# First norm in a hand-written order with its gain spread by TensorE, the conv result kept as a high/low pair in DRAM, and the up projection with its second accumulator first

## The chip, the cores and the metric

The kernel runs on one core of a Trainium2 chip. Such a core has five engines that work side by side, each through its own list of instructions: PE (TensorE, matmul), DVE (VectorE), ACT (ScalarE), POOL (GpSimd) and SP (SyncE, which here issues nearly all DMAs). The metric is the device time of one execution in microseconds. Lower is better.

## The reference

One transformer block on a sequence of 1024 tokens with 1024 features, all in float32:

```python
h = rms_norm(x, norm1_g)
z = h @ w_in                                 # 1024 x 7168
glu_in, q, k, v, gate_logits = split(z)
a = a_val * sigmoid(a_gate)                  # the halves of glu_in
a = causal_depthwise_conv(a, conv_w, conv_b) # 31 taps
a = silu(rms_norm(a, conv_norm_g))
y_a = a @ w_conv_out
o = dilated_window_attention(rms_norm(q), rms_norm(k), v)   # 16 heads, three window groups mixed
y_b = o @ w_attn_out
g_a, g_b = split(sigmoid(gate_logits + gate_b))
x = x + (g_a * y_a + g_b * y_b) @ w_out
h = rms_norm(x, norm2_g)
u = causal_depthwise_conv(h @ w_up, ffn_conv_w, ffn_conv_b) # 3 taps, width 2 x 2816
x = x + (silu(u_gate) * u_val) @ w_down
```

## The kernel before

Every float32 operand of a matmul is split into a rounded high part and the rest, low: `split` (L74) issues the high as a copy on ACT (L76) and the low as a subtraction on DVE (L77). A product is then three matmuls: high x high, high x low, low x high (L108 to L110). Weights come in pieces of 128 x 1024 (512 KB): `stage` loads one into a ring of four buffers, `wsplit` splits it into rings of four high and four low buffers, and `wpiece` does both.

The program is one long list, written in the order of the stages; a scheduler then puts each engine's instructions in an order that follows their dependences and the program order. Memory is handed out in pools, and a tile that takes over memory of an earlier one waits for that one's last user, a DMA included.

- First norm (L197 to L224). The gain g1 is loaded as a broadcast to 128 partitions (`gb1`). For each of eight tiles of 128 tokens: Square with a running sum on ACT, mean and epsilon on DVE, power -0.5 on POOL (`rstd_of`, L98), a scale on DVE (L223), eight transposes on PE (L190), two splits into `hT`.
- GLU (L227 to L238). Per channel of 128 a gate product `glug` and a value product `gluv`, 48 matmuls each.
- q, k, v products, meanwhile the depthwise conv on DVE (`conv_branch`, L242): 31 instructions of 128 x 1024 for each of eight channels.
- Gate products, drawn from the generator `gate_steps` (L146) as cover for PE: 24 steps before the conv's sum of squares, 16 before its spread (`psr`, L333), and 52 behind the loop L336 to L340, which scales each conv channel (DVE), applies Silu (ACT) and writes it to DRAM, `da`, by a DMA on SP's queue (`COVER`, L36). Each gate piece is loaded as `raw_gt`, split into `hi_gt` and `lo_gt`; ACT brings the result out as `gs` (L151).
- Attention (L345 to L470). `head` loads q, kh, kl, mask m and v of a head (L133); `score` (L378), `flip` and `weigh` work on it a head half at a time. Between them `fill` takes steps from `side_work`: the remaining gates, then the projection `ya` of the conv branch, whose input `aT` is read back from `da` in eight pieces and split again by `load_split` (L165).
- Merge, output projection and second norm (L473 to L543): `wo` products by tile of 128 tokens, the norm's steps, transposes (`transpose_raw`, L509) two tiles later.
- Up projection (L557 to L659). The product of 1024 x 1024 by 1024 x 256 (f-th columns of value and gate) is made with seven products of half-size blocks in place of eight. The blocks of the normed input are b11, b12, b21, b22, their sums t1 to t4 (`sums`, L594, with subtractions on POOL), each split. `up_first` makes the first two products into the accumulators X and Z, `up_sums` the sums of the weights, `up_rest` the remaining five products, into X and Y, and the conv and Silu.
- Down projection (L664 on), likewise in blocks.

## Time and profile before

| | |
|---|---|
| time, median of 3 runs | 1813.47 us (1812.62 to 1814.06) |
| profiled execution | 1811.43 us |
| its span, from first to last instruction | 1809.6 us |
| mean granted clock of PE | 0.991 of full speed |
| busy: PE, DVE, ACT, POOL | 1765.8, 1318.8, 771.6, 195.8 us |
| instructions | 22474 |
| HBM read, written | 190.03 MB, 66.06 MB |

All times within the profile count from the start of the span. A timeline row gives an instruction's start and duration, then engine, line (L76 is line 76 of the kernel), operation, tile written <- tiles read, shape and number of instructions, and in brackets how long the engine stood idle before it and what it then waited for. "SPq" and "ACTq" mark the issue of a DMA. The landing time is from the issue to the DMA's end. Durations of PE's rows are those of single matmuls, which overlap; how far apart the starts are is what one costs.

### The profile page before, as it was taken

To read this page: it belongs to the slowest core of one execution; us is meant where nothing else is said; L and a number is where in the kernel's file an instruction comes from. 1 tells how busy PE (TensorE), PEld (TensorE's weight loads), DVE (VectorE), ACT (ScalarE), POOL (GpSimd) and SP (SyncE) were. 2 spreads that over 40 slices of the span, in tenths; PEclk is the share of its full clock that TensorE was granted. 3 is DMA by queue.
4 is the path that set the end of the run, shared out by engine and by line. 5 is a ranking of instruction groups with operands and counts; after the bars stand their busy time and mean duration, and the time that the engine had idled before them with its cause. 6 is when DMAs were issued, how large, how long until landed. Compare 5 with 4: busy or idle time off the path is not lost.

```text
span 1809.6 us, 22474 instructions
## 1 busy us (share of the span) xinstructions
PE 1765.8 (98%) x8244; PEld 1461.9 (81%) x8244; DVE 1318.8 (73%) x1798; ACT 771.6 (43%) x1202; POOL 195.8 (11%) x197
## 2 busy tenths in 40 slices
PE   7999999999999999999999999989999999999999
PEld 5888888888887888887888878768888888878887
DVE  5999999999735655666654543787777777789863
ACT  4111132232245656666655332545444554543441
POOL 1000133133002122222210000210000000000000
PEclk9999999999999999999999999999999999999999
DMA  5111145345549456666527543313222222389851
GB/s 203 59 47 47 41 134 163 116 134 157 157 173 246 145 158 175 180 165 179 164 70 279 169 160 133 104 48 107 80 82 81 71 95 91 116 303 335 298 180 47
DMA packets 142063, 257.57 MB, mean 142 GB/s; under 512 B 11265, under 2 KB 60545, under 8 KB 141953
## 3 DMA queue, kind: packets, MB, share of 16 engines
q1 hardware_dynamic: 141808, 255.61, 43.8%
q8 instruction: 65, 1.06, 0.3%
q10 hardware_dynamic: 144, 0.52, 0.1%
q14 instruction: 46, 0.37, 0.1%
HBM read 190.03 MB, written 66.06 MB: 142 GB/s over the span
## 4 chain that ended last, share of the span: by engine, by line
PE 53%; DMA 4%; DVE 4%; issue 1%; ACT 1%; SPq 1%; POOLq 0%; POOL 0%; DVEq 0%; ACTq 0%
PE xz L550 5%; PE xz L551 5%; PE xz L552 5%; PE dx L703 5%; PE dy L703 5%; DMA gg<-dya 2%; PE pp L400 2%; PE y L550 2%; PE y L552 2%; PE y L551 2%; PE ya L108 2%; PE ya L109 2%; PE ya L110 2%; PE o L408 2%; PE wo L126 1%; PE wo L127 1%
## 5 line engine op out<-in xcount | busy, mean ns | idle before, releaser
L253 DVE SCALAR_TENSOR_TENSOR cacc<-apad,pk,cacc 128x1024 f32<-128x1024 f32 x240 | 297.7, 1274 | 0.7
L125 PE MATMUL qkv<-hi_qkv,hT 128*128 128x512 f32 x384 | 151.8, 396 | 0.0
L127 PE MATMUL qkv<-hi_qkv,hT 128*128 128x512 f32 x384 | 150.0, 391 | 0.0
L126 PE MATMUL qkv<-lo_qkv,hT 128*128 128x512 f32 x384 | 149.4, 390 | 0.0
L389 DVE CUSTOM_DVE_ANT_0 p<-s,m 128x128 f32<-128x128 f32 (+7 forms) x128 | 95.1, 750 | 62.7 <-PE pp L400 39.0
L77 DVE TENSOR_TENSOR pl<-pp,ph 128x512 fp32r<-128x512 f32 x192 | 103.1, 549 | 49.1 <-ACT ph L76 48.6
L393 POOL TENSOR_SCALAR p<-p,st 128x128 f32<-128x128 f32 (+7 forms) x128 | 94.9, 748 | 335.5 <-DVE st L392 211.9
L76 ACT ACTIVATE ph<-pp 128x512 fp32r<-128x512 f32 x192 | 91.3, 487 | 92.2 <-PE pp L400 89.3
L649 DVE SCALAR_TENSOR_TENSOR u<-u,pk 128x1023 f32<-128x1023 f32 (+1 forms) x88 | 112.3, 1279 | 18.9 <-ACT u L647 18.5
L101 POOL TENSOR_TENSOR rs<-ss,mhalf 128x8 f32<-128x8 f32 (+1 forms) x40 | 80.3, 2010 | 353.1 <-DVE ss L100 353.0
L391 ACT ACTIVATE p<-p,st 128x128 f32<-128x128 f32 (+7 forms) x128 | 99.0, 776 | 14.6 <-DVE st L389 12.9
L108 PE MATMUL gate<-hT,hi_gt 128*128 128x512 f32 x256 | 101.8, 398 | 0.0
L109 PE MATMUL gate<-hT,hi_gt 128*128 128x512 f32 x256 | 100.8, 394 | 0.0
L110 PE MATMUL gate<-hT,lo_gt 128*128 128x512 f32 x256 | 100.3, 393 | 0.0
L400 PE MATMUL pp<-ident,p 128*128 128x128 f32 x576 | 94.4, 277 | 0.0
L127 PEld LDWEIGHTS qkv<-hi_qkv,hT 128*128 128x128 f32 x384 | 72.0, 188 | 15.3
L126 PEld LDWEIGHTS qkv<-lo_qkv,hT 128*128 128x128 f32 x384 | 72.2, 188 | 14.5 <-DVE lo_qkv L77 0.3
L125 PEld LDWEIGHTS qkv<-hi_qkv,hT 128*128 128x128 f32 x384 | 72.2, 188 | 14.0
L400 PEld LDWEIGHTS pp<-ident,p 128*128 128x128 f32 x576 | 69.5, 142 | 10.0 <-issue 0.2
L384 PE MATMUL s<-kh,q 128*128 128x512 f32 (+1 forms) x192 | 69.7, 368 | 7.3 <-DVE st L389 4.8
L408 PE MATMUL o<-ph,v 128*128 128x512 f32 x192 | 73.1, 381 | 3.6 <-ACT ph L76 1.8
L409 PE MATMUL o<-pl,v 128*128 128x512 f32 x192 | 70.5, 369 | 1.6 <-DVE pl L77 1.5
(269 smaller groups left out, 4610.4 us busy)
## 6 DMA issues: line engine op xcount, KB each, us to landing
wr<-w_down SPq DMA_DIRECT2D x45, 512.0 KB, 5.7
gr<-dff SPq DMA_DIRECT2D x62, 256.0 KB, 5.2
raw_qkv<-w_qkv SPq DMA_DIRECT2D x24, 512.0 KB, 3.9
raw_uv<-w_up SPq DMA_DIRECT2D x22, 512.0 KB, 3.3
raw_ug<-w_up SPq DMA_DIRECT2D x22, 512.0 KB, 3.3
dff<-u SPq DMA_DIRECT2D x22, 512.0 KB, 2.6
dv<-v SPq DMA_DIRECT2D x16, 512.0 KB, 3.2
raw_gt<-w_ch SPq DMA_DIRECT2D x16, 512.0 KB, 4.8
```

The costliest lines, as they stand in the source:

```text
L108: pe.matmul(o, hi[:, k, :], ah[:, k, :], start=(k == 0), stop=False)
L109: pe.matmul(o, hi[:, k, :], al[:, k, :], start=False, stop=False)
L110: pe.matmul(o, lo[:, k, :], ah[:, k, :], start=False, stop=(k == KT - 1))
L125: pe.matmul(ps, ah, hi[:, k % 2, :], start=(k == 0), stop=False)
L126: pe.matmul(ps, ah, lo[:, k % 2, :], start=False, stop=False)
L127: pe.matmul(ps, al, hi[:, k % 2, :], start=False, stop=(k == KT - 1))
L253: dve.scalar_tensor_tensor(out=acc, in0=a[:, j : j + T], scalar=w(j), in1=acc, op0=ALU.mult, op1=ALU.add)
L400: pe.transpose(pp[:, qb * P : (qb + 1) * P], pts[qb][:, kt * P : (kt + 1) * P], ident)
L550: pe.matmul(o, wh[:, k, :], bh[:, k, :], start=(start and k == 0), stop=False, skip_group_check=not start)
L551: pe.matmul(o, wh[:, k, :], bl[:, k, :], start=False, stop=False, skip_group_check=not start)
L552: pe.matmul(o, wl[:, k, :], bh[:, k, :], start=False, stop=(k == 3), skip_group_check=not start)
L703: pe.matmul(banks[n], a[:, c], b[:, d], start=(start and i == 0 and m == 0), stop=(stop and i == nf - 1 and m == 2), skip_group_check=True)
```

## The change

Three stages are rewritten; the matmuls stay the same, but for two.

First norm and first GLU channel: g1 comes as one row of 4 KB and is spread over the partitions by two matmuls with ones. ACT, DVE and PE follow an order written by hand: four Squares first, powers a tile ahead of the scales, and the products of the first channel, gate and value for one half of the tokens at a time, are taken high x high first, in between the transposes of the second half.

Conv result: after Silu each channel is split into a high and a low tile in the ring `t4` (four buffers), and both are written to DRAM, `da[0]` and `da[1]`. `aT` is then fetched in four DMAs of 2 MB, with no split behind them.

Second norm and up projection: an order written by hand for ACT, DVE and PE from the last norm tiles to the first up products; the first two up weights are loaded and split ahead of it; all block sums are on DVE, none on POOL. In `up_rest` the products into Y come ahead of those into X, and the two buffers of `u` are swapped.

```diff
-    da = dr.tile([P, KT, T], F32, name="da")
+    da = [dr.tile([P, KT, T], F32R, name=f"da{a}") for a in range(2)]
...
-        gb1 = p1.tile([P, D], F32, tag="csq", bufs=1, name="gb1")
-        act.dma_start(gb1, bass.AP(tensor=g1.tensor, offset=g1.offset, ap=[[0, P], [1, D]]))
+        g1r = p1.tile([1, D], F32, tag="csq", bufs=1, name="g1r")
+        act.dma_start(g1r, g1.unsqueeze(0))
...
-                wfirst = [wpiece(w_ch[8], "g0"), wpiece(w_ch[0], "v0")]
+                wfirst = [(c, n, stage(w_ch[c], n)) for c, n in ((8, "g0"), (0, "v0"))]
...
-            act.activation(xs, xx, AF.Square, accum_out=ss)
-            rstd_of(rs, ss, D, ss)
-            dve.scalar_tensor_tensor(out=xs, in0=xx, scalar=rs, in1=gb1, op0=ALU.mult, op1=ALU.mult)
-            transpose_split(hT, xs, tt)
...
+        gb1 = p1.tile([P, D], F32, tag="sqacc", bufs=1, name="gb1")
+        xn = [t4(f"xs_{tt}") for tt in range(4)]
+        st1 = p1.tile([P, 2, 8], F32, name="st1")
+        tps = {}
+
+        def squares(tt):
+            if tt >= 4:
+                xn.append(t4(f"xs_{tt}"))
+            act.activation(xn[tt], xt[tt], AF.Square, accum_out=st1[:, 0, tt : tt + 1])
+
+        def spread1(tt):
+            rstd_of(st1[:, 1, tt : tt + 1], st1[:, 0, tt : tt + 1], D, st1[:, 0, tt : tt + 1])
+
+        def scaled(tt):
+            dve.scalar_tensor_tensor(out=xn[tt], in0=xt[tt], scalar=st1[:, 1, tt : tt + 1], in1=gb1,
+                                     op0=ALU.mult, op1=ALU.mult)
+
+        def turned(tt):
+            for kk in range(2):
+                ps = third[:, kk * 512 : kk * 512 + 512] if tt == 2 else bank_ps(f"tp_{tt}_{kk}")
+                for j in range(4):
+                    k = kk * 4 + j
+                    pe.transpose(ps[:, j * P : (j + 1) * P], xn[tt][:, k * P : (k + 1) * P], ident)
+                tps[tt, kk] = ps.rearrange("p (a b) -> p a b", a=4)
...
+        HH, HL, LH = ((0, 0),), ((0, 1),), ((1, 0),)
+        with tc.manual_schedule(engines={ENG.Activation, ENG.DVE, ENG.PE}):
+            ps = [bank_ps(f"gb_{kk}") for kk in range(2)]
+            for kk in range(2):
+                pe.matmul(ps[kk], ones[0:1, :], g1r[:, kk * 512 : kk * 512 + 512], start=True, stop=True)
+            for tt in range(4):
+                squares(tt)
+            dve.tensor_copy(gb1[:, 0:512], ps[0])
+            spread1(0)
+            dve.tensor_copy(gb1[:, 512:1024], ps[1])
+            spread1(1)
+            for tt in range(4):
+                scaled(tt)
+                turned(tt)
+                if tt < 2:
+                    spread1(tt + 2)
+                if tt == 2:
+                    both(0, 0)
+            both(0, 1)
+            both(1, 0)
+            both(2, 0)
...
+            act.activation(hl[0][0], wraw[0], AF.Copy)
+            both(3, 0)
+            act.activation(hl[1][0], wraw[1], AF.Copy)
+            wlow(0)
+            wlow(1)
+            a, b = range(4), range(4, 8)
+            first_pair(0, a, HH, 0)
+            first_pair(0, a, HH, 1)
+            first_pair(0, a, HL + LH, 0)
+            first_pair(0, a, HL + LH, 1)
+            squares(4)
+            spread1(4)
...
+            glu0[1] = big_ps("glugv_1")
+            both(6, 1)
+            ends = both(7, 1)
...
-            sp.dma_start(da[:, c, :], ct)
+            pair = [t4(f"a{h}_{c}", F32R) for h in range(2)]
+            split(*pair, ct)
+            for h in range(2):
+                spill(da[h][:, c, :], pair[h])
         for _ in range(COVER[2]):
             next(gates)
 
 
     with tc.tile_pool(name="ph2", bufs=1) as p2:
+        def take(aT, half):
+            for h in range(2):
+                fetch(aT[h][half], da[h][:, :, half * 512 : half * 512 + 512])
+
         def side_work():
             for t in gates:
                 if t == "half":
                     aT = hb_tiles(hb1, "aT")
-                    load_split(aT, da, 0, "a")
+                    take(aT, 0)
                 yield
-            load_split(aT, da, 1, "a")
+            take(aT, 1)
...
                 gemm_tok(ps, mT, wpieces, tt)
-                dve.tensor_tensor(out=x2[:, cs], in0=ps, in1=x2[:, cs], op=ALU.add)
-                sp.dma_start(dx2[tt][:, cs], x2[:, cs])
-                act.activation(ps, x2[:, cs], AF.Square, accum_out=ss2[:, tt, j : j + 1])
+                if j == 1 and tt == 7:
+                    break
+                add_rest(j, tt, x2, ps)
...
-            pool.tensor_tensor(out=t1, in0=b12[:, :, q], in1=b11[:, :, q], op=ALU.subtract)
-            dve.tensor_tensor(out=t3, in0=b22[:, :, q], in1=b12[:, :, q], op=ALU.subtract)
-            keep("t3", t3, q)
-            dve.tensor_tensor(out=t3, in0=t3, in1=b11[:, :, q], op=ALU.add)
-            keep("t2", t3, q)
-            keep("t1", t1, q)
...
+        pre = [stage(w_up[f], f"uv{f}") for f in range(2)]
+        pre = [(v, wsplit(v, f"uv{f}")) for f, v in enumerate(pre)]
+        t2 = [p4r.tile([P, 1024], F32, tag="st", bufs=2, name=f"cb_t2_{i}").rearrange("p (a b) -> p a b", a=4)
+              for i in range(2)]
+        order = tc.manual_schedule(engines={ENG.Activation, ENG.DVE, ENG.PE})
+        order.__enter__()
         transpose_raw(*tails.pop(0))
+        add_rest(1, 7, x2, ps)
+        transpose_raw(*tails.pop(0))
+        q0, q1 = cols
+        less(t13[0], b12[:, :, q0], b11[:, :, q0])
+        s7 = spread(7)
+        high2("t1", t13[0], q0)
+        less(t2[0], b22[:, :, q0], t13[0])
+        scale2(x2, s7)
+        low2("t1", t13[0], q0)
+        v0, xz0 = up_first(0, pre[0])
+        transpose_raw(x2, 7)
         assert not tails
+        weights = up_sums(0, v0)
+        next(weights)
+        ups = [up_first(1, pre[1])]
 
     with tc.tile_pool(name="ph4", bufs=1) as p4:
-        for n in ("b22", "t4"):
-            blocks[n] = p4.tile([P, 2, 4, 512], F32R, name=f"blk_{n}")
-        ups = [up_first(1)]
-        sums(cols[1])
-        for q in cols:
-            keep("b22", b22[:, :, q], q)
-        for i, q in enumerate(cols):
-            pool.tensor_tensor(out=t2[i], in0=b21[:, :, q], in1=t2[i], op=ALU.subtract)
-            keep("t4", t2[i], q)
-        blk = {n: (t[:, 0], t[:, 1]) for n, t in blocks.items()}
+        half4 = lambda pl, n, **k: pl.tile([P, 4, 512], F32R, name=f"blk_{n}", **k)
+        blocks["b22"] = half4(p4, "b22h"), half4(p4, "b22l")
+        high2("b22", b22[:, :, q0], q0)
+        less(t13[1], b12[:, :, q1], b11[:, :, q1])
+        high2("t1", t13[1], q1)
+        less(t2[1], b22[:, :, q1], t13[1])
+        low2("t1", t13[1], q1)
+        high2("b22", b22[:, :, q1], q1)
+        s4 = [four(t) for t in wsplit(v0[:, 512:], "s4_0")]
+        low2("b22", b22[:, :, q0], q0)
+        low2("b22", b22[:, :, q1], q1)
+        for q, t in zip(cols, t2):
+            high2("t2", t, q)
+        for q, t in zip(cols, t13):
+            less(t, b22[:, :, q], b12[:, :, q])
+        for q, t in zip(cols, t2):
+            last = low2("t2", t, q)
+        order.__exit__(None, None, None)
+        sw, gw, _ = next(weights)
+        ready = [(v0, xz0, sw, gw, s4)]
+        with tc.issue_after(last.ins):
+            for q, t in zip(cols, t13):
+                high2("t3", t, q)
+                low2("t3", t, q)
+            blocks["t4"] = half4(p4, "t4h"), half4(p4r, "t4l", tag="t13", bufs=1)
+            for t, q in zip(t2, cols):
+                less(t, b21[:, :, q], t)
+                high2("t4", t, q)
+                low2("t4", t, q)
+        blk = blocks
...
-            u = hb2.tile([P, 4, T], F32, tag=f"hb{f % 2}0", name=f"u_{f}")
+            u = hb2.tile([P, 4, T], F32, tag=f"hb{(f + 1) % 2}0", name=f"u_{f}")
             uv, ug, cv, cg = u[:, 0], u[:, 1], u[:, 2], u[:, 3]
             p5 = cst.tile([P, 512], F32, tag="f2", bufs=2, name=f"p5_{f}")
-            X, Z = xz[:, 0:512], xz[:, 512:1024]
+            X, Z = xz
             Y = bank_ps(f"y_{f}")
             t0, t1 = slice(0, 512), slice(512, 1024)
             (sh, sl), (gh, gl) = sw, gw
             act.activation(uv[:, t0], X, AF.Copy)
             dve.tensor_tensor(out=uv[:, t0], in0=Z, in1=uv[:, t0], op=ALU.add)
+            product(Y, sh[:, 0:4], sl[:, 0:4], *blk["t1"], True)
+            act.activation(p5, Y, AF.Copy)
+            s4h, s4l = s4 if f == 0 else [four(t) for t in wsplit(s4, f"s4_{f}")]
+            product(Y, s4h, s4l, *blk["b22"], False)
             product(X, sh[:, 4:8], sl[:, 4:8], *blk["t2"], False)
             act.activation(uv[:, t1], X, AF.Copy)
-            product(Y, sh[:, 0:4], sl[:, 0:4], *blk["t1"], True)
-            act.activation(p5, Y, AF.Copy)
             product(X, gh[:, 0:4], gl[:, 0:4], *blk["t3"], False)
             dve.tensor_tensor(out=ug[:, t1], in0=X, in1=p5, op=ALU.add)
-            s4h, s4l = [four(t) for t in wsplit(s4, f"s4_{f}")]
-            product(Y, s4h, s4l, *blk["b22"], False)
             dve.tensor_tensor(out=uv[:, t1], in0=Y, in1=uv[:, t1], op=ALU.add)
```

More of the change, by code (lines that the diff above doesn't have):

```diff
@@ L227, in block_kernel @@
+        for ks in (a, b):
+            for which in range(2):
+                first_pair(1, ks, HH + HL + LH, which)
+        with tc.issue_after(ends[1].ins):
+            dve.tensor_tensor(out=qkg, in0=pk[:, C_QG : C_QG + 1], in1=pk[:, C_KG : C_KG + 1], op=ALU.mult)
+            dve.tensor_scalar(qkg, qkg, DH ** -0.5, None, op0=ALU.mult)
+        with tc.issue_after(ends[0].ins), tc.issue_after(ends[1].ins):
+            wsecond = [wpiece(w_ch[9], "g1"), wpiece(w_ch[1], "v1")]
         apad = []
```

164 lines of the change are left out of this document (107 added, 57 removed).

## The prediction

> **What bounds the kernel now.** I read the page first: busy times and the slices.
>
> ```profile
> PE 1765.8 (98%) x8244; PEld 1461.9 (81%) x8244; DVE 1318.8 (73%) x1798; ACT 771.6 (43%) x1202; POOL 195.8 (11%) x197
> ...
> PE   7999999999999999999999999989999999999999
> ```
>
> TensorE (PE) is busy 1765.8 us of a span of 1809.6, so 43.8 us of idle, and some time at a low clock, are all that an edit can win unless it removes matmuls; this one adds two small ones. The time is in a few seams, which the windows view shows (columns: stretch, length, busy time of PE, PE weight load, DVE, ACT, POOL, granted PE clock, DMA share, GB/s).
>
> ```profile
> core 0: us, PE busy (x) PEld busy (x) DVE busy (x) ACT busy (x) POOL busy (x), PEclk, DMA share, GB/s
> 0.00:20.00 20.00, 6.95 (x32) 5.57 (x32) 10.82 (x17) 13.01 (x23) 3.65 (x18) 0.92 0.93 357
> 550.00:600.00 50.00, 48.80 (x253) 40.94 (x253) 28.75 (x84) 30.20 (x68) 13.93 (x20) 0.94 0.82 228
> 800.00:820.00 20.00, 17.13 (x87) 14.19 (x86) 14.97 (x35) 15.31 (x30) 5.16 (x7) 0.89 0.90 258
> 1150.00:1200.00 50.00, 40.76 (x181) 32.08 (x181) 47.90 (x46) 27.87 (x38) 14.03 (x6) 0.93 0.22 72
> ```
>
> 13.05 us idle lie in the first 20 us (the first norm), 2.87 at 800 to 820 (before the conv branch's output projection, ya), 9.24 at 1150 to 1200 (second norm into the up projection), where DVE is busy 47.90 of 50. The change works at these three seams, and it puts new work before a fourth: the start of attention near 547. Between the seams PE is full, so time won at one reaches the end unless a later seam takes it back.
>
> The profiled execution took 1811.43, 2.04 below the median of 1813.47; I sum against the former and add 2 at the end.
>
> **Part 1, the first norm (gain).** The timelines of PE, ACT, DVE and POOL (columns: start, duration, what, in brackets the idle time before and its releaser), then the landing of the broadcast gain (size, median), that of the eight conv spills da (shortest, median, longest), and the rate of all DMA in 40 slices of the first 20 us:
>
> ```profile
> 9.41 4.03 PE L190 MATMUL tp<-ident,xs 128*128 128x128 f32 x16 [9.41 <-DVE ss L100]
> 20.18 0.80 PE L108 MATMUL glug<-hT,hi_g 128*128 128x512 f32 x1 [0.48 <-ACT hT L76]
> 23.94 0.39 PE L109 MATMUL glug<-hT,hi_g 128*128 128x512 f32 x1
> 48.21 0.50 PE L108 MATMUL glug<-hT,hi_g 128*128 128x512 f32 x1
> ...
> 5.99 1.06 ACT L221 ACTIVATE xs<-x 128x1024 f32<-128x1024 f32 x1 [3.55 <-DMA x<-x]
> ...
> 8.07 1.28 DVE L223 SCALAR_TENSOR_TENSOR xs<-x,rs,gb 128x1024 f32<-128x1024 f32 x1 [0.75 <-POOL rs L101]
> 18.13 1.22 DVE L77 TENSOR_TENSOR lo_v<-raw_v,hi_v 128x1024 fp32r<-128x1024 f32 x1
> ...
> 7.48 0.56 POOL L101 TENSOR_TENSOR rs<-ss,mhalf 128x1 f32<-128x1 f32 x1 [6.04 <-DVE ss L100]
> ...
> 506.43 0.61 PE L333 MATMUL psr<-dg,ones 128*128 128x128 f32 x4
> 546.79 0.39 PE L109 MATMUL gate<-hT,hi_gt 128*128 128x512 f32 x1
> 547.02 0.39 PE L110 MATMUL gate<-hT,lo_gt 128*128 128x512 f32 x1
> ...
> gb<-g ACTq DMA_DIRECT2D x1, 512.0 KB, 5.5
> ...
> DMA to landing us min/median/max: 2.6/3.1/7.0
> ...
> GB/s 0 0 0 98 205 229 270 311 336 401 311 401 434 402 418 426 418 418 418 418 426 418 418 418 418 434 410 418 426 410 434 434 393 391 428 437 401 426 410 434
> ```
>
> Today the 512 KB broadcast runs ahead of x. At 418 GB/s that is 1.25 us; with a 4 KB row in its place the x tiles land that much earlier, and the first Square starts at 4.74 instead of 5.99. From Square to power took 1.49 (7.48 - 5.99), from power to scale 0.59 (8.07 - 7.48): by x alone the first scale could start at 6.8. The gain comes through two fp32 matmuls: psr's four of 128 columns took 0.61 at the full clock, so with their tail 0.9 for 512 columns, and 1.7 at the head's clock (the eight steps from 20.18 to 23.94 are 0.47 each, against 0.23 between 546.79 and 547.02), and two copies, of which the last, some 0.7 (a little over half of 1.22), stands behind them. If the row g1r lands 2.6 after its issue near 0.7, as the quickest of da's, that is 3.3 + 3.4 + 0.7 = 7.4, which I take; with the broadcast's 5.5 it would be 10.3. Four scales then follow, each tile's power beside the scale before: 4 x 1.28 and 0.6 for the small steps (read and multiply, within the 0.43 that 1.49 leaves beside the Square), 13.1. With four transposes and one high the first product starts near 15.5, against 20.18. The weight splits and tiles 4 to 7 then lie beside PE work: the 48 products of tiles 0 to 3 for the first channel take 48 x 0.23 and some 2 for the clock, 13 us, while the last x lands at 4.74 + 9 x 1.25 = 16.0. So no later stall. Gain 5 (4 to 6; 2 if g1r lands last): the second channel's first product moves from 48.21 to about 43.2. From there to 500 PE is full, and the gain lasts.
>
> What speaks against it is the power of one tile on POOL beside the scale of another on DVE. Where a power met a split on DVE (two inputs from SBUF) at the second norm, it was stretched:
>
> ```profile
> 1158.24 1.40 POOL L101 TENSOR_TENSOR s<-s,mhalf 128x1 f32<-128x1 f32 x1 [9.12 <-DVE s L100]
> ```
>
> 1.40 against 0.56. In the new head the powers of tiles 2 and 3 are asked for just as a scale starts. If each waits the scale out and then runs, the next scale starts some 0.65 late (0.56 and a hand-over), 1.3 in all, and the gain is 3.7 instead of 5. That is the second rival below; for the sum I keep 5, as three of the four scales may find the power done. The Trainium skill, "SBUF — State Buffer" (Terms, shared port pair), has it as a rule: DVE and GpSimd lock the port pair that they share for a whole instruction, and the loser is blocked until its end. By that rule the head gains 3.7; the 1.40 agrees with it.
>
> **Part 2a, the conv pair before attention (loss).** The timelines of PE, ACT and SP, and SP's waits (total, times, longest):
>
> ```profile
> 549.63 0.77 PE L384 MATMUL s<-kh,q 128*128 128x128 f32 x2 [2.22 <-DMA kl<-dk]
> ...
> 547.22 1.06 ACT L76 ACTIVATE hi_gt<-raw_gt 128x1024 fp32r<-128x1024 f32 x1 [4.48 <-PE gate L109]
> 548.18 0.67 ACT L151 ACTIVATE gs<-gate,pk 128x512 f32<-128x512 f32 x1
> ...
> 531.24 2.23 SPq L340 DMA_DIRECT2D da<-cacc x2
> 539.58 0.52 SPq L133 DMA_DIRECT2D q<-dq x1
> ...
> SPq L133 <- DMA da<-cacc: 4.7, 2, 3.5
> ```
>
> The last gate product ends at E = 547.4 (547.02 + 0.39). Head 0's loads reuse the memory of the conv tiles, so SP issues the first (539.58) only when the last da spill has landed; the spill went out by 533.5. The first score comes 10.05 after the first load, 2.2 after E: nearly in time, because the last spill follows straight on the last Silu.
>
> In the changed order eight highs (ACT, 1.06 as hi_gt) and eight lows (DVE, 1.22) come between Silu and spill, 16 spills go out instead of 8, and a ring of four buffers allows two pairs in flight, so each pair waits for the spills of the pair two before. What decides is the order: on ACT, the high of channel 6 stands behind that hi_gt, and the high of channel 7 behind the last gs. hi_gt stood 4.48 for the gate weights' use on PE, that is until E - 0.2; gs waits for the last gate product itself. So, after E: hi_gt to 0.9, high 6 to 1.9, gs to 2.5, high 7 to 3.5, low 7 (1.22) to 4.7, spill issued. It lands 2.6 to 7.0 later; behind six other transfers of the same queue I take 4.5: E + 9.2. SP holds head 0's loads, and all behind them, for it. The first score came 10.05 after the first load; with less on the DMA, down to 7. I take 8.5: E + 17.7, against E + 2.2: loss 15.5 (bounds: 4.7 + 2.6 + 7 - 2.2 = 12 and 4.7 + 7 + 10.05 - 2.2 = 19.5). PE has nothing else here: the gate cover ahead is as long as before, and the later gate work is woven between scores. The idle costs no more clock than before: 0.94 over 550 to 600 is a cold start already.
>
> **Part 2b, the pair read back (gain).** The PE timeline, and the operations on the tile aT (count, shortest, median and longest ns, first and last start):
>
> ```profile
> 814.45 0.33 PE L408 MATMUL o<-ph,v 128*128 128x128 f32 x1 [1.30 <-ACT ph L76]
> 816.32 0.47 PE L409 MATMUL o<-pl,v 128*128 128x128 f32 x1 [1.54 <-DVE pl L77]
> 820.02 0.63 PE L108 MATMUL ya<-aT,hi_co 128*128 128x512 f32 x1
> ...
> L76 ACT ACTIVATE aT<-raw_a x8: 1042/1059/1070, 760.0 to 813.2; 128x1024 fp32r<-128x1024 f32 x8
> L77 DVE TENSOR_TENSOR aT<-raw_a,aT x8: 1214/1220/1225, 761.2 to 814.8; 128x1024 fp32r<-128x1024 f32 x8
> ```
>
> The second four of these splits, up to 816, stand ahead of the last head's ph and pl, for which PE waits 1.30 + 1.54; the clock of 0.89 over these 20 us is another 2. The splits go; four 2 MB fetches replace the eight loads; the w_co loads move from 812 into the heads before. The last head's chain keeps some wait. Gain 4.5 (3 to 6). The fetches take some 5 us of the DMA's time each and go through SP's queue ahead of head loads, which are a head early: nothing, or up to 2 at a DMA share of 0.90.
>
> **Part 3, second norm into up (about nothing).** PE and POOL timelines and DVE's groups of 1156 to 1200:
>
> ```profile
> 1179.88 0.80 PE L551 MATMUL y<-blk_t,hi_s 128*128 128x512 f32 x1 [4.70 <-DVE blk_t L77]
> ...
> 1169.94 3.05 POOL L599 TENSOR_TENSOR cb_t<-h2raw,h2raw 128x1024 f32<-128x1024 f32 x1 [3.56 <-ACT h2raw L516]
> ...
> L540 DVE SCALAR_TENSOR_TENSOR x<-x,s,gb 128x1024 f32<-128x1024 f32 x2 | 4.7, 2344 | 0.0
> L602 DVE TENSOR_TENSOR cb_t<-cb_t,h2raw 128x1024 f32<-128x1024 f32 x2 | 4.0, 2004 | 0.0
> L77 DVE TENSOR_TENSOR lo_s<-raw_uv,hi_s 128x512 fp32r<-128x512 f32 x2 | 3.6, 1788 | 0.0
> L571 DVE TENSOR_TENSOR s<-raw_ug 128x512 f32<-128x512 f32 x2 | 3.4, 1716 | 0.0
> ```
>
> The four POOL subtractions go to DVE: 4 x 1.22 = 4.9 more. Each of them had stretched one DVE operation; against 1.28, 1.22, 0.68 and 0.68 undisturbed the four groups hold 2.1 + 1.6 + 2.2 + 2.0 = 8 too much, which comes back. DVE, the bound here, has 3 less. But the order written by hand makes waits of its own: the last norm tile's transposes wait for its sum, power and scale; the second half's t2, t3 and t4 splits come ahead of the sums for f = 1, whose s1 products come right behind f = 0's b22. Going through the instructions in the new order with these durations I get PE waits of 0.6, 1.1, 6.0, 0.8 and 1.3, 9.8 in all beside some 1.5 at the last transposes, against 9.24 idle today; and PE's matmuls are then further on. Net gain 1, between -1.5 and 3. The swap of the u buffers and Y before X in every later f moves nothing while PE is full.
>
> **Sum.** -5 + 15.5 - 4.5 - 1 = +5 on 1811.43, 1816.4; with 2 for the median 1818.5. Its own range: loss 12 to 19.5, gains 13 to 8, so 1813 to 1823.
>
> **Rivals.**
> Faster: the spill tail drains within the gates. The pairs are only 8 x 1.06 on ACT and 8 x 1.22 on DVE, some 10 us side by side, and today's last spill goes out 14 before E; were ACT not held by hi_gt and gs, the last would land by E, the loss would be 0 to 6, and the time 1803 to 1809. Against it is the order on ACT and the 4.48. It decides at whether high 7 runs before E. Chance 0.15.
> The lock: head gain 3.7, 1820. Chance 0.15.
> A wash: tail at its lower bound (12), head 6, ya 6 and transition 1: 1812.5 after the median's 2. Chance 0.13.
> Worse: the DMA backs up. 16 spills are 8.4 MB, 20 us at 418 GB/s, beside gate loads and spills; with landings at 7 and loads at 10 (19.5), a late g1r (gain 2) and ya 3: 1811.4 + 19.5 - 2 - 3 + 2 = 1828. Chance 0.12. It decides at a last da landing later than 7 after issue.
> The change doesn't do what it says, because g1r lands as late as the broadcast did: inside the ranges above.
>
> **Numbers.** Forecast 0.45. 0.2% of this time, 3.6 us, is what a measurement can tell from no change; so faster is below 1809.8, slower above 1817.1. Faster: 0.15 + 0.05 of the wash = 0.2. Same: 0.08 of the wash and 0.12 of the forecast's lower end = 0.2. Slower: 0.33 + 0.15 + 0.12 = 0.6. The range, 1808 to 1825, takes in the wash and the near ends of the faster and the worse case.
>
> **What would show it.** First product at 15.5 and the second channel's at 43: part 1 right. PE idle of 12 to 18 between the last gate matmul and the first score, released by a DMA of head 0, with the last da spill issued some 5 after the last gate: part 2a right; the first score within 5 of the gates' end would refute it and make the whole faster. No wait over 1 for ph and pl before ya: 2b. One PE wait near 6 for hi_s of f = 1: part 3. If every term is as given but the total is off, a clock or a DMA wait elsewhere was missed.

## The result, and the profile after

The changed kernel takes 1836.21 us (median of 4 runs, 1832.62 to 1836.77), against 1813.05 (4 runs, 1811.24 to 1814.06) for the kernel before on the same chip: a ratio of 1.0125, 95% interval 1.0107 to 1.0142. It is slower, as predicted, but by 23 us instead of 5, and outside the range. The profiled execution took 1832.62, its span is 1830.8, 21.2 longer than before.

First the busy times of the page after; then the windows that answer to those of before:

```profile
PE 1771.1 (97%) x8248; PEld 1460.8 (80%) x8248; DVE 1317.3 (72%) x1805; ACT 772.6 (42%) x1203; POOL 183.9 (10%) x193
```

```profile
0.00:20.00 20.00, 14.29 (x53) 9.77 (x54) 13.03 (x20) 13.33 (x22) 5.14 (x19) 1.00 0.87 339
550.00:600.00 50.00, 34.05 (x163) 27.89 (x164) 20.24 (x58) 21.04 (x48) 9.85 (x14) 0.76 0.73 196
1150.00:1200.00 50.00, 41.59 (x199) 33.13 (x198) 40.49 (x48) 28.08 (x41) 4.07 (x4) 0.95 0.22 74
```

The work is the same; the idle has moved. PE is busy 14.29 of the first 20 us instead of 6.95, but from 550 to 600 it is busy 34.05 at a clock of 0.76, where it was 48.80 at 0.94. PE's waits in the changed kernel (total, times, longest; rows with a part in the argument):

```profile
PE s L503 <- DMA kh<-dk: 22.1, 1, 22.1
...
PE y L681 <- ACT hi_s L76: 5.7, 1, 5.7
PE dx L868 <- ACT gh_b L76: 3.0, 1, 3.0
PE xz L681 <- ACT u L803: 2.7, 2, 1.6
...
PE dx L868 <- ACT u L808: 1.4, 1, 1.4
```

One wait, before the first score of attention, is 22.1, where it was 2.2 before: a difference nearly as large as the whole loss. The waits for `u` and `gh_b` lie in the last quarter, where the prediction had put nothing at all.

To find where time comes and goes I follow the same matmul through the traces: its start less its start in the kernel before. In the table a term of the sum is the step from one column to the next; times at the top are those of before. (psr: spread of the conv's norm. score 0 and s_2_3: the first and a later score of attention. ya: in the first half of the conv's projection. wo: the middle of the output projection. y_4, y_20: last product into Y for f = 4 and 20. dy: late in the down projection. At each of the last five the same number of products has run before it in every run, but for the four matmul records that spread the gain.)

| run | psr 506.4 | score 0 549.6 | s_2_3 589.7 | ya 884.2 | wo 1110.9 | y_4 1262.4 | y_20 1567.0 | dy 1791.4 |
|---|---|---|---|---|---|---|---|---|
| after | -6.3 | +13.6 | +17.4 | +12.6 | +10.5 | +8.6 | +12.4 | +20.9 |
| e1 head only | -6.5 | -5.6 | -5.3 | -5.9 | -2.1 | -0.8 | -0.8 | -0.8 |
| e2 pair only | +1.5 | +22.2 | +26.3 | +21.3 | +21.9 | +21.9 | +21.9 | +22.3 |
| e3 up only | -0.1 | +1.1 | +2.0 | +2.3 | +0.8 | -0.5 | +2.9 | +15.8 |
| e4 u unswapped | -6.4 | +13.7 | +16.9 | +11.8 | +10.2 | +12.2 | +12.2 | +12.5 |
| e5 low in place | -6.3 | +8.6 | +12.8 | +8.3 | +6.9 | +5.2 | +9.9 | +16.7 |
| e6 swap only | +0.3 | +0.9 | +0.8 | +0.8 | +0.7 | 0.0 | +1.9 | +6.0 |
| e7 head and pair, new order | -6.4 | +13.7 | +17.0 | +12.2 | +10.3 | +10.3 | +10.3 | +10.3 |
| e8 all, both mended | -6.0 | +14.1 | +17.8 | +12.8 | +10.4 | +13.1 | +13.1 | +13.6 |
| e9 double spill | -0.1 | +12.0 | +16.4 | +15.4 | +19.0 | +18.9 | +18.9 | +19.4 |
| e10 high only | -6.3 | +2.1 | +4.9 | +0.1 | -1.3 | -2.1 | +2.5 | +10.0 |
| e11 X first | -6.8 | +13.5 | +16.5 | +11.2 | +14.3 | +12.9 | +14.8 | +21.0 |
| e12 head and up, unswapped | -6.4 | -6.5 | -6.5 | -7.3 | -6.7 | -3.9 | -3.9 | -3.4 |

The changed kernel's row reads: head -6.3, start of attention +23.7, ya -4.8, transition -1.9, up projection +3.8, start of the down projection +8.5. The step from ya to wo, -2.1, is no term: it lies between -2.4 and +3.8 in the other rows without regard to the edits (e1 +3.8, e9 +3.6, e11 +3.1), a seam that varies from run to run. In e1 and e9 PE waits 4.2 and 4.0 at the start of the output projection for its split weights, against 2.8 before and 1.0 after; over the 20 us from there the granted clock is 0.83 and 0.85, in the other two 1.00. So a single profile is good to about 4 us, and the medians of several runs decide.

**The head.** Timelines of PE, DVE and POOL, changed kernel:

```profile
2.32 3.75 PE L254 MATMUL gb<-g1r,ones 1*128 1x512 f32 x4 [2.32 <-DMA g1r<-g]
6.91 1.29 DVE L217 SCALAR_TENSOR_TENSOR xs<-x,st,gb 128x1024 f32<-128x1024 f32 x1
6.94 0.55 POOL L100 TENSOR_TENSOR st<-st,mhalf 128x1 f32<-128x1 f32 x1 [0.78 <-DVE st L99]
9.12 1.28 DVE L217 SCALAR_TENSOR_TENSOR xs<-x,st,gb 128x1024 f32<-128x1024 f32 x1
9.28 1.53 POOL L100 TENSOR_TENSOR st<-st,mhalf 128x1 f32<-128x1 f32 x1 [0.85 <-DVE st L99]
10.85 1.28 DVE L217 SCALAR_TENSOR_TENSOR xs<-x,st,gb 128x1024 f32<-128x1024 f32 x1 [0.36 <-POOL st L100]
16.20 1.20 PE L246 MATMUL glugv<-hT,whi_g 128*128 128x512 f32 x4 [0.96 <-ACT hT L233]
41.70 0.39 PE L107 MATMUL glug<-hT,hi_g 128*128 128x512 f32 x1
```

The row g1r is there at 2.32, the first scale starts at 6.91, the first product at 16.20 instead of 20.18, the second channel's at 41.70 instead of 48.21. Between the first two scales lie 2.21 instead of 1.28: in the order written by hand the small step for tile 2 stands ahead of the second scale, and it waits 0.84 for tile 2's Square, which waits 1.33 for its x to land. The fourth scale, at 12.65, ends at 13.93.

**The start of attention.** Timelines of PE, ACT, DVE and SP of the changed kernel:

```profile
540.77 0.39 PE L109 MATMUL gate<-hT,lo_gt 128*128 128x512 f32 x1
563.23 0.76 PE L503 MATMUL s<-kh,q 128*128 128x128 f32 x2 [22.07 <-DMA kh<-dk]
...
540.97 1.06 ACT L76 ACTIVATE hi_gt<-raw_gt 128x1024 fp32r<-128x1024 f32 x1 [3.53 <-PE gate L108]
542.32 1.06 ACT L76 ACTIVATE a<-cacc 128x1024 fp32r<-128x1024 f32 x1 [0.29 <-DMA da<-a]
543.28 0.67 ACT L150 ACTIVATE gs<-gate,pk 128x512 f32<-128x512 f32 x1
545.45 1.06 ACT L76 ACTIVATE a<-cacc 128x1024 fp32r<-128x1024 f32 x1 [1.50 <-DMA da<-a]
...
546.70 1.23 DVE L77 TENSOR_TENSOR a<-cacc,a 128x1024 fp32r<-128x1024 f32 x1 [1.91 <-DMA da<-a]
...
545.06 3.27 SPq L129 DMA_DIRECT2D da<-a  x3
554.36 0.51 SPq L132 DMA_DIRECT2D q<-dq  x1
```

Who waited for the spills to land there, in the view of the tensor da (us, times), and SP's own wait for the last (total, times, longest):

```profile
  DVE a L77: 5.9, 4
  ACT a L76: 3.3, 3
```

```profile
SPq L132 <- DMA da<-a: 5.8, 1, 5.8
```

and the group of the eight spills before (issue shortest, median and longest in ns, first and last start):

```profile
L340 SPq DMA_DIRECT2D da<-cacc x8: 319/320/1277, 523.5 to 532.6; - x8
```

The last gate product ends at E = 541.2 (540.77 + 0.39). On ACT the order is the one that the prediction had worked out: hi_gt, the high of channel 6, gs, the high of channel 7. But the ring is full: the last two highs wait 0.29 and 1.50 for the landing of the earlier spills whose buffers they take, and the last low, which waits for a buffer too, follows at 546.70. The last three spills are issued at 545.06, 546.53 and 547.96 (the row merges them); each issue takes SP 0.32 to 0.43, and between them SP waits for high and low. The sixteen spills land 2.6 to 7.8 us after their issue, in the median 6.0; the last at 554.08, 6.1 after. The first load of head 0 goes out at 554.36, the first score starts at 563.23, E + 22.1. Granted clock in the ten us from the first score on, before and after (columns as in the windows of the prediction):

```profile
549.60:559.60 10.00, 8.77 (x30) 6.70 (x31) 5.40 (x19) 5.52 (x13) 3.20 (x6) 0.67 1.03 268
```

```profile
563.20:573.20 10.00, 7.72 (x19) 5.57 (x20) 2.37 (x12) 3.69 (x9) 2.13 (x4) 0.50 1.03 260
```

The granted clock in the ten us after a wait of 2.22 was 0.67, after one of 22.07 it was 0.50. That is a part of the 3.8 between score 0 and s_2_3: over that whole stretch the mean granted clock is 0.92 for 40.1 us before and 0.88 for 43.9 after, which makes some 2 us by estimate, and PE is idle 2.8 there instead of 1.2.

**Up and down projection.** Waits of ACT for the writing of `u` to DRAM from 1190 to 1600, before and after:

```profile
ACT u L631 <- DMA dff<-u: 4.8, 4, 2.3
```

```profile
ACT u L796 <- DMA dff<-u: 15.2, 6, 4.0
```

The end of the up projection, timelines of PE and SP in the changed kernel, and SP's wait there; then the timeline of SP at the same place before:

```profile
1606.29 0.39 PE L868 MATMUL dx<-hi_a,early 128*128 128x512 f32 x1
1611.73 0.39 PE L681 MATMUL xz<-blk_t4h,hi_s3g 128*128 128x512 f32 x1
...
1614.64 0.34 SPq L876 DMA_DIRECT2D res<-dx  x1
1617.58 4.50 SPq L841 DMA_DIRECT2D gr<-dff  x7
```

```profile
SPq L876 <- PE xz L683: 8.3, 1, 8.3
```

```profile
1594.71 1.76 SPq L711 DMA_DIRECT2D res<-dx  x4
1596.52 4.62 SPq L676 DMA_DIRECT2D gr<-dff  x7
```

The last X product of f = 21 (`t4`, 12 matmuls) now stands behind 24 products of the down projection. The loads `res` wait 8.3 for it in SP's queue, and the loads `gr` behind them go out 11.3 after the first down product (1617.58 - 1606.29); before, they went out 2.0 after it (1596.52 against 1594.47). PE then waits 3.0 for `gh_b` and 1.4 for `u`. Every run with the buffers swapped has these 24 products ahead of the last X product and the `gr` loads 10.2 to 11.3 after the first down product; every run with them unswapped has 0 and 2.0 to 2.1.

### The profile page after: what moved, and what is told of

Same layout as the page of the kernel before. It is cut to its first block, busy times and chain, and to the rows that moved or that the text cites. A ratio compares the mean times of both kernels' runs of the same rounds, so it can differ in the third digit from the quotient of the medians.

```text
span 1830.8 us, 22492 instructions
## 1 busy us (share of the span) xinstructions
PE 1771.1 (97%) x8248; PEld 1460.8 (80%) x8248; DVE 1317.3 (72%) x1805; ACT 772.6 (42%) x1203; POOL 183.9 (10%) x193
## 4 chain that ended last, share of the span: by engine, by line
PE 50%; DMA 5%; DVE 4%; issue 1%; ACT 1%; SPq 1%; DVEq 0%; ACTq 0%
PE xz L681 5%; PE xz L683 5%; PE xz L682 5%; PE dx L868 5%; PE dy L868 3%; PE pp L519 2%; PE y L681 2%; PE y L682 2%; PE y L683 2%; DMA gg<-dya 2%; PE ya L107 2%; PE ya L108 2%; PE ya L109 2%; PE wo L125 2%; PE wo L126 2%; PE wo L124 2%
## 5 line engine op out<-in xcount | busy, mean ns | idle before, releaser
L100 POOL TENSOR_TENSOR rs<-ss,mhalf 128x8 f32<-128x8 f32 x32 | 73.8, 2311 | 337.9 <-DVE ss L99 337.9
L503 PE MATMUL s<-kh,q 128*128 128x512 f32 (+1 forms) x192 | 69.1, 365 | 28.9 <-DMA kh<-dk 22.1
L126 PEld LDWEIGHTS qkv<-hi_qkv,hT 128*128 128x128 f32 x384 | 72.1, 188 | 15.5
```

The source lines that it names most:

```text
L126: pe.matmul(ps, al, hi[:, k % 2, :], start=False, stop=(k == KT - 1))
```

## The experiments

The kernel before, timed beside them, took 1812.6 to 1814.2 (medians). The theory that the first ones test: the pair costs by its wait at the start of attention, and the swap of the `u` buffers costs at the end of the up projection. The rival: the loss comes from one interaction, and parts alone cost little.

### The parts alone, and the swap undone

**e1** is the kernel before with the new first norm and GLU head, nothing else.

> The kernel before with the new first norm alone. Theory (the parts add up): the second GLU channel's first product starts near 42.2 instead of 48.21, and the whole is 6 us faster than before, at 1807. Rival (the head's gain is lost again at the conv's end, where DVE and not PE is late): as before, within 1 us of 1813.

Measured 1806.23 (1804.46 to 1810.62), ratio 0.9958 (0.9941 to 0.9975): 7 faster. The profiled run is the slowest of the four, and lost its 4 at the varying seam before wo; up to ya it is 5.9 ahead. The head's gain is real and reaches the end.

**e2** is the kernel before with the pair alone:

```diff
-            sp.dma_start(da[:, c, :], ct)
+            pair = [t4(f"a{h}_{c}", F32R) for h in range(2)]
+            split(*pair, ct)
+            for h in range(2):
+                spill(da[h][:, c, :], pair[h])
```

and with `take` in place of `load_split`.

> The kernel before with the high/low pair of the conv result alone. Theory: first score 20 us or more after the last gate product, 23 us lost there with the cold clock, 5 won before the conv branch's projection: 18 us slower, 1831. Rival (the wait at attention was so long only because the new head moved the conv's end): a loss of 15 there, 1823.

Measured 1832.48 (1829.28 to 1833.96), 1.0104 (1.0089 to 1.0119): 19 slower. PE waits 23.0 before the first score, and the table has +24.8 from psr to s_2_3, -5 to ya.

**e3** is the kernel before with the new second norm, transition and up projection, the swap among them.

> The kernel before with the second norm and up projection rewritten alone. Theory (this part, put at -1 in the prediction, costs time in the up projection and at its end): 1.5 won up to the first products of f = 2, then 5 lost over the up projection and 6 at the start of the down projection: 9 us slower, 1822. Rival (those losses come from the other two parts, which shift the DMAs): 1 to 3 us faster, 1811.

Measured 1826.61 (1818.51 to 1827.52), 1.0064 (1.004 to 1.0088): 14 slower, more than the 9 expected. The transition gains 1.3 (wo to y_4), the up projection loses 3.4, the start of the down projection 12.9. So the third part, forecast at -1, loses, and where no term stood. Alone the three parts make -7, +19 and +14, +26 together, near the 23 of the whole: the rival of an interaction falls.

**e4** is the changed kernel with one edit:

```diff
-            u = hb2.tile([P, 4, T], F32, tag=f"hb{(f + 1) % 2}0", name=f"u_{f}")
+            u = hb2.tile([P, 4, T], F32, tag=f"hb{f % 2}0", name=f"u_{f}")
```

> The changed kernel with the two buffers of u taken in the order of before, one index changed; Y stays first. Theory (the swapped buffers make u wait for the write of the f before, and put the last product of f = 21 behind the first down products, with the loads of gr behind it): the loads of gr go out 8 to 10 us earlier against the first down product, the up projection loses nothing, and the time falls by 8 to 11 us, to 1825 to 1828. Rival (Y ahead of X is what costs there): the same as the changed kernel, within 2 us of 1836.

Measured 1828.49 (1824.13 to 1828.85), 1.0079 (1.0063 to 1.0094): 8 faster than the changed kernel. From y_4 on its row is flat (+12.2 to +12.5). The timeline of SP at the end of the up projection, where the first down product starts at 1606.68:

```profile
1608.68 5.16 SPq L841 DMA_DIRECT2D gr<-dff  x7
```

The loads `gr` go out 2.0 after it again instead of 11.3, as expected. The swap has a use too: without it PE waits 2.8 at the transition for `lo_s`, the granted clock from 1190 to 1215 is 0.73 instead of 0.86, and that step goes from -1.9 to +2.0. The balance is a loss.

### The swap alone, and the order of the products

**e6** is the kernel before with the swap of the `u` buffers alone.

> The kernel before with nothing changed but which of its two buffers u takes first. Theory (the swap by itself turns the order of the last products and delays the loads of the down projection): last product of f = 21 behind the first down products, loads of gr 8 to 10 later against them, 8 to 12 us slower, 1821 to 1825. Rival (it hurts only together with the new order of the products and sums): within 2 us of 1813.

Measured 1820.33 (5 runs, 1817.45 to 1827.31), 1.0048 (1.0029 to 1.0066): 8 slower than the 1812.62 of before beside it, at the lower edge of what was expected. PE's waits show the two that the changed kernel has:

```profile
PE xz L550 <- ACT u L634: 2.5, 2, 1.4
...
PE dx L703 <- ACT u L643: 1.4, 1, 1.4
```

ACT waits 17.8 for the writes of `u` (4.8 before), and here too the last X product stands behind the first down products. An edit that moves no work and changes only which of two buffers comes first costs some 8 us.

**e11** is the changed kernel with the products of every f from 1 on in the old order (X before Y), the buffers swapped as in the change.

> The changed kernel with the products of f = 1 and on in the order of before, X's t2 ahead of Y's, with u's buffers swapped as in the change. Theory (Y first adds some 5 to the cost of the swap): 1830 to 1832. Rival (only the swap costs): 1835 to 1837. A second rival (Y first is what costs, and the unswapped buffers only hid it): 1824 to 1827.

Measured 1833.29 (1828.2 to 1834.37), 1.0098 (1.0079 to 1.0117): between the two expectations, 3 less than the changed kernel, which the spread of the runs doesn't separate from nothing. From y_4 on it loses 8.1, the changed kernel 12.3, e6 6.0. Y before X adds a little to the swap; how much is open. In e4, with Y first and the buffers unswapped, it costs nothing.

### What makes the wait before attention

The prediction had put the wait on the order on ACT: the last highs stand behind hi_gt and gs, which wait for the last gate product. Its rival "worse" put it on the DMA. The next five tell these apart.

**e5** is the changed kernel with the low part written over the conv tile, so that only the highs go through the ring:

```diff
-            pair = [t4(f"a{h}_{c}", F32R) for h in range(2)]
-            split(*pair, ct)
-            for h in range(2):
-                spill(da[h][:, c, :], pair[h])
+            ah = t4(f"a0_{c}", F32R)
+            split(ah, ct.bitcast(F32R), ct)
+            spill(da[0][:, c, :], ah)
+            spill(da[1][:, c, :], ct)
```

> The changed kernel with the low half of each conv channel written over the conv tile itself, so that the ring t4 holds only highs: four channels in flight instead of two, and the last high goes before the last gate weights' split. Theory (what holds attention is that the last pair comes behind the gates, because of the ring): the last spill is issued before the last gate product ends, the first score comes 5 to 9 us after it instead of 22, and the time falls by 13 to 17, to 1819 to 1823. Rival (the DMA queue backs up with 16 spills whatever the order): first score still 18 or more after, 1832 to 1836.

Measured 1829.68 (1828.39 to 1830.66), 1.0094 (1.0077 to 1.0111): 6.5 less than the changed kernel, where 13 to 17 were expected. The timeline of SP, and PE's wait:

```profile
542.09 1.05 SPq L129 DMA_DIRECT2D da<-cacc  x1
...
548.97 0.51 SPq L132 DMA_DIRECT2D q<-dq  x1
```

```profile
PE s L503 <- DMA kl<-dk: 17.1, 1, 17.1
```

No high or low waits for the ring any more and the last spill goes out at 542.09, 1 after the gates' end and 6 earlier than in the changed kernel; but it takes 6.9 until head 0's first load, and PE still waits 17.1. The last high ran at 534.52, well ahead of the gates' end, and still 14.9 of the 19.9 that the changed kernel loses up to the first score remain. The ring, and the order on ACT that it brings with it, is a part, the smaller one.

**e7** is e1 with the pair in e5's form and the conv's end in an order by hand: all scales and Silus first, then all splits and spills.

> The kernel before with the new first norm and with the pair, the low in place and the conv's end for ACT and DVE in an order written by hand, highs right behind the eight Silus. Theory: 7 us from the head and 5 before the conv branch's projection stay, attention loses 0 to 6: 1801 to 1807, faster than before and than the head alone by up to 5. Rival (the spills still hold the first loads): 1815 or more.

Measured 1822.91 (1821.55 to 1826.49), 1.0058 (1.0043 to 1.0073). The first theory falls here. With all Silus first, the first spill goes out at 526.8 instead of 519.2; the wait before the first score is 22.3, and 23.4 are lost up to s_2_3, as in the changed kernel (23.7). Timelines of DVE and SP:

```profile
537.47 1.23 DVE L77 TENSOR_TENSOR cacc<-cacc,a 128x1024 fp32r<-128x1024 f32 x1 [1.45 <-ACT a L76]
...
546.52 1.02 SPq L129 DMA_DIRECT2D da<-cacc  x1
```

The last low is done at 538.70, 2.3 before the gates' end, but SP comes to its spill only 7.8 later, for each issue ahead of it takes about 1. No high or low holds it any more.

**e8** is the changed kernel with e7's conv end and e4's unswapped buffers.

> All parts of the change, with the conv's end as in the run before this one and u's buffers in the order of before. Theory (losses at attention and in the up projection are independent): 1836 - 8 - 16 = 1812, between 1808 and 1814, 3 to 6 slower than the run before this one, since u's first tile then waits longer at the second norm. Rival (mending one exposes the other): above 1818.

Measured 1824.54 (1823.01 to 1826.9), 1.0065 (1.005 to 1.008). 1812 was expected, and it is missed for the reason that e7 shows: the new conv end leaves the wait at 22.3. What the swap cost is gone (flat from y_4 on), what the pair costs is not.

**e9** is the kernel before with the DMA load of the pair and none of its work: each conv channel is written a second time, to a tensor that nothing reads.

```diff
             sp.dma_start(da[:, c, :], ct)
+            sp.dma_start(da2[:, c, :], ct)
```

> The kernel before with each conv channel written to DRAM twice, the second time to a place that nobody reads: the DMA load of the pair without its ACT and DVE work and without its ring. Theory (the DMA is full between conv and attention, 0.99 of its time from 530 to 541 in the changed kernel): 8 more spills of 1.25 us hold the first loads by 8 to 11, 8 to 12 slower, 1821 to 1825. Rival (ACT, DVE and the ring hold the pair): the queue drains within the gates, 1813 to 1816.

Measured 1829.67 (1826.33 to 1831.85), 1.0082 (1.0064 to 1.0099): 15.5 slower, where 8 to 12 were expected, with not one instruction more on PE, DVE or ACT. The same window in the kernel before and in e9, e9's issues (shortest, median and longest in ns), the timeline of SP, and PE's wait:

```profile
530.00:541.00 11.00, 11.00 (x50) 9.11 (x49) 1.23 (x1) 4.46 (x6) 0.00 (x0) 1.00 0.76 267
```

```profile
530.00:541.00 11.00, 11.00 (x50) 9.11 (x49) 1.23 (x1) 4.46 (x6) 0.00 (x0) 1.00 1.05 388
```

```profile
L341 SPq DMA_DIRECT2D da<-cacc x8: 320/1121/1152, 523.4 to 540.2; - x8
```

```profile
541.36 1.40 SPq L342 DMA_DIRECT2D da<-cacc  x1
...
550.01 0.52 SPq L133 DMA_DIRECT2D q<-dq  x1
```

```profile
PE s L386 <- DMA kh<-dk: 14.3, 1, 14.3
```

The DMA is full (1.05 of its engines' time and 388 GB/s, against 0.76 and 267 before), the last spill goes out at 541.36 instead of 532.6, and it is 8.6 until the first load. Of these 8.6 the landing takes 7.2; in the rest SP's queue stands at a load of gate weights that waits for `lo_gt`. Up to s_2_3 e9 loses 16.5, the changed kernel 23.7. The median landing of these spills is 5.6, against 3.1 for the eight of before.

**e10** is the changed kernel with half the spills: it leaves out the writes of the low parts, and the highs are read in their place:

```diff
-            for h in range(2):
-                spill(da[h][:, c, :], pair[h])
+            spill(da[0][:, c, :], pair[0])
...
-                fetch(aT[h][half], da[h][:, :, half * 512 : half * 512 + 512])
+                fetch(aT[h][half], da[0][:, :, half * 512 : half * 512 + 512])
```

> The changed kernel with high and low made as there, but only the high written to DRAM, and read back for both (the low part of the conv result is replaced by the high). The ACT and DVE work of the pair without its DMA load. Theory (DMA): first score within 6 of the last gate product, 15 to 18 faster than the changed kernel, 1818 to 1821. Rival (the work and its order on ACT and DVE): first score 15 or more after, 1830 or more.

Measured 1824.13 (1821.68 to 1828.07), 1.006 (1.0041 to 1.0079): 12 less than the changed kernel, where 15 to 18 were expected. Timelines of SP and PE:

```profile
534.35 2.17 SPq L129 DMA_DIRECT2D da<-a  x3
542.72 0.51 SPq L132 DMA_DIRECT2D q<-dq  x1
...
551.70 0.77 PE L502 MATMUL s<-kh,q 128*128 128x128 f32 x2 [10.56 <-DMA kh<-dk]
```

All highs and lows are still made, but the last spill is out by 536.5, 4.6 before the gates end. The first score comes 10.56 after the gates' end, between the theory's 6 and the rival's 15. Up to s_2_3 11.2 are lost, of 23.7. So the splits and the traffic each cost alone (11.2 and 16.5), and together less than their sum, for both put off the same event, the landing of the last spill.

### The rest without the pair

**e12** is the changed kernel without the pair and with the buffers unswapped.

> The changed kernel without the pair and with u's buffers in the order of before: new first norm, new second norm, all block sums on DVE, Y first. Theory (the rewritten second norm costs 2 where u's first tile waits): 1806 + 2, 1807 to 1810. Rival (it wins what it was put at): 1804 to 1806, level with or better than the head alone.

Measured 1808.08 (5 runs, 1804.65 to 1809.41), 0.9958 (0.9944 to 0.9973). As expected, and level with the head alone (1806.23; both ratios are 0.9958): the rewritten second norm and up projection lose 2.8 from wo to y_4 in the trace, with these waits of PE:

```profile
PE y L674 <- ACT hi_s L76: 5.7, 1, 5.7
...
PE y L676 <- DVE lo_s L77: 2.8, 1, 2.8
```

So all that the change wins over the kernel before, 0.4%, comes with the head alone, which is 1.6% faster than the changed kernel (1806.23 against 1836.21). That the rest adds nothing is shown only within the intervals of e1 and e12.

## Why the prediction was right and wrong

**Part 1, the head: right.** Forecast -5 (4 to 6); measured -6.0 to -6.8 in the traces of the runs that have the new head, and -7 in e1's median. The path is the forecast one, its times differ a little, both ways. g1r landed at 2.32 instead of 3.3 and the first scale started at 6.91 instead of 7.4. But the four scales ended at 13.93 instead of 13.1, for the second one waited for x of tile 2, and the first product, which waited 0.96 for a high on ACT, came at 16.20 instead of 15.5. The second channel's first came at 41.70, not 43.2: 25.5 after the first channel's, where it was 28.0 before. The lock, the second rival, is there, once: the power at 9.28 took 1.53 beside the scale that ran from 9.12 to 10.40. The Trainium skill, "SBUF — State Buffer" (Terms, shared port pair), says that the loser is blocked for the whole instruction. This row agrees with it; the two other powers that started within 0.03 of a scale, at 6.94 and 10.84, took 0.55 and show no block. The price was 0.36 of waiting before one scale, not 1.3, for DVE had been busy until just before.

**Part 2a, the pair before attention: right place, too small, and the cause is only a part of it.** Forecast 15.5 (12 to 19.5), measured 23.7. By the prediction's own steps, four terms were mis-sized or put at nothing. The last spill was to go out at E + 4.7, and SP issued it at E + 6.8 (547.96), since the last high and low wait for the ring, which waits for landings, a wait that the prediction names but gives no time: +2.1. It was to land 4.5 after its issue; the first load came 6.4 after (554.36 - 547.96): +1.9. From first load to first score 8.9 against 8.5: +0.4. And "The idle costs no more clock than before" was wrong: 3.8 more are lost up to s_2_3, about half of it by the clock as estimated above, the rest mostly as idle time of PE in that stretch. 2.1 + 1.9 + 0.4 + 3.8 = 8.2, the whole difference. The 4.5 stood against the trace of before itself: there the last spill went out at 532.6 and the first load at 539.58, 7.0 later. The rows show a shortest of 2.6, a median of 3.1 and a longest of 7.0, and the one that counts, the last in the queue, is close to the longest. I took a value from the middle for a quantity that is near the maximum.

What the runs say of the cause: the prediction had the highs' order on ACT decide. That order stands in the trace, but undoing it doesn't undo the loss. In e5 and e10 the last high ran before the gates' end, the very condition of the "faster" rival, which then gave a loss of 0 to 6; up to the first score it was 14.9 and 8.4, up to s_2_3 19.1 and 11.2. In e7 all highs and lows were done 2.3 before the gates' end, and nothing was won. In e9 no work was added and 16.5 were lost. What decides is when the last spill lands, for SP holds head 0's loads until then (5.8 in the changed kernel). Two things put that landing off: twice the bytes, with the DMA full, issues of about 1 us and landings of 5 to 8 (e9, e7), and the splits with their order (e10). For scale: 8.4 MB at e9's 388 GB/s are 21.6 us of the DMA's time, before any gate transfer. Nearest to it came the rival "worse" at 12%, with the wrong sign by which to know it: I had said that it decides at a last landing later than 7 after its issue. The last one took 6.1; the backlog showed earlier, in landings of up to 7.8, which held the ring.

**Part 2b, the read back: right.** Forecast -4.5 (3 to 6); s_2_3 to ya -4.8, in e2 -5.0, and no wait over 1 for ph and pl is left. In e1 and e9, where the pair isn't read back, that step is -0.6 and -1.0.

**Part 3: the transition right by its number, in part by luck, the rest wrong.** Forecast -1 with one wait near 6 for hi_s; measured -1.9, with a wait of 5.7. In e3 -1.3. But the gain hangs on the swap, which the forecast had put at nothing: without it the same order loses 2.0 (e4), 2.7 (e8) and 2.8 (e12), with a wait of 2.8 for lo_s that is not among the five of the prediction. What failed is one sentence: "The swap of the u buffers and Y before X in every later f moves nothing while PE is full". It cost 12.3 (3.8 and 8.5), in the medians some 8 net of what the swap gains at the transition (1836.21 against e4's 1828.49). The swap is needed for it: e4 has 0.3 there. The order of the instructions changed with it; SP's queue then carried the wait from one late product of X to the loads of the down projection. I had priced the swap by its work, none, and not looked at what the scheduler made of it, though that order comes from the scheduler and is the same in every run with the swap. The prediction's last line, "a clock or a DMA wait elsewhere was missed", names a part of what happened.

**Sum.** Forecast -5 + 15.5 - 4.5 - 1 = +5; measured -6.3 + 23.7 - 4.8 - 1.9 + 12.3 = +23.0, less the 2.1 of the varying seam, +20.9. The forecast's own range was also added up wrong: 1813.4 with a loss of 12 to 19.5 and gains of 13 to 8 gives 1812.4 to 1824.9, not 1813 to 1823. The measured time lies beyond either.

Open: why the steady order of the up projection differs by the buffer that `u` starts with (the writes of `u` come 4.0 and 34.0 apart by turns before, 10.3 and 28.1 in the changed kernel; what first shifts them wasn't followed); the share of Y before X; and why the split weights come late at the seam before wo in some runs.

## What to carry to other kernels

Where a transfer releases memory for the next stage, price it by its last landing, at the load that the stage itself puts on the DMA: count the bytes from the first spill to the release, and read the longest landing of the trace before, not the median. Here twice the bytes written ahead of such a release cost 15.5 us though no engine had more work (e9). An edit that only renames a buffer can be an edit of the order, here one of 8 us (e6): compare the instruction order at the next seam, DMA queue included, before calling it nothing.

## What the runs showed of the hardware that was not expected

With the DMA full the issue itself slows: a spill of 512 KB took SP 0.32 in the median of the eight before and 1.12 in the median of e9's first ones of each pair, so a backlog holds SP's queue too; e7 shows the price, a finished tile that waited 7.8 for its issue. And the granted clock was lower after the longer idle time: in the ten us after it, it was 0.67 after 2.22 of waiting and 0.50 after 22.07.
